# Transposing w for seven heads with VectorE and DMAs in place of TensorE, in a hybrid attention layer

## The chip, the cores and the metric

The kernel runs on one core of one Trainium2 chip. Its time is the device time of one execution in microseconds (us); lower is better. The kernel before takes 351.91 us, the median of three runs (351.11 to 352.12).

## The reference, cut to what matters

A layer over 512 positions with 1024 features, all in f32. The input is normalised and projected; eight heads use stick-breaking attention ("sb") and eight use block attention with slopes ("mb"). With 512 positions and blocks of 256, all past blocks are selected, so an mb head is a causal softmax with a linear position term. Each half of the heads is normalised, gated and projected out, and a gate with a side input closes the layer.

```python
q_sb, k_sb, v_sb, z_sb, q_mb, k_mb, v_mb, z_mb = jnp.split(rmsnorm(x, g_mix) @ w_in, split_at, axis=-1)
# mb head: s = q k^T * scale - slope * (q_pos - k_pos), masked to the past
probs = softmax(s)
out = probs @ v
y_mb = rmsnorm(o_mb, g_out_mb) * silu(z_mb)
x = x + concat([y_sb, y_mb]) @ w_out
x = x + (p @ w_ple) * sigmoid(rmsnorm(x, g_ple) @ w_ple_gate)
return rmsnorm(x, g_final)
```

## The kernel before

Nothing is rounded to fewer bits than needed: each f32 operand of a product is split into a hi part (fp32r, a cast on ScalarE, `part_hi`, L80) and a lo part (VectorE subtracts hi from the source, `part_lo`, L86), and a product is three matmuls, hi hi, hi lo and lo hi (`mul3`, L75). Weights come by DMA into three raw tiles, are split into `wu` tiles (five of them), and the next load is issued when a lo part has freed a raw tile.

TensorE's order is written out by hand. A stream of projection steps (`F`, three matmuls each) runs through the whole attention stage; the work of the heads is put between these steps. A slot belongs to head h (loop at L764): the transposes of head h-1's w, the scores of head h (`scores`, L590, eight matmuls into one three-bank PSUM tile `sc`, which has one buffer), the sums of head h-1 (`sums`, L701), and projection steps between them and after them up to a number `TARGET[h]`. The tail (L816 to L832) does the transposes and sums of head 15 between the last steps.

For an mb head (`front_mb`, L640) VectorE takes the row maxima of scores plus positions (`top`, L648, four operations that read `sc`), ScalarE the exponentials (L656), VectorE the reciprocal of the row sums and four scalings of w by it (`norm`, L664). The positions `rel` are halved per head (L642). w has 1280 columns in 128 partitions: four row blocks, of 512, 384, 128 and 256 columns, the causal part alone. `trans` (L685) transposes ten 128x128 blocks on TensorE into PSUM, in three groups of 4, 4 and 2 blocks, and splits each group into `ph` and `plo`. `sums` multiplies V with both. `turn` (L879) is used in the last stage for x2: VectorE transposes 32x32 blocks within a tile, one DMA writes the tile to DRAM, four DMAs bring it back with the blocks at their transposed places.

The orders of VectorE, ScalarE, GpSimd and SP are not written by hand after the start: a scheduler sets them when the program is built, with its own estimates of when inputs are ready and with priority for some. Each engine runs its row in that order and waits where an input is missing.

Of the kernel before, what the change touches and what calls it, by code (L numbers as in the profile page):

```python
# [20 lines left out]
NH = 8  # L21
# [13 lines left out]
def layer(ctx, tc, x, xT, pT, w_qkz, w_v, gcols, g_final, w_out, w_ple, w_gate, out):  # L35
# [100 lines left out]
    def flush_f():  # L136
        while fq:
            pop_f()
# [221 lines left out]
    def end_v(g, t, ps):  # L360

        ps = ps.rearrange("p (r e d) -> p r e d", r=2, e=2)
        hi = V[g][t][:, :, 0::3, :]
        part_hi(hi, ps, rx["t"][:, t:t + 1])
        for r in range(2):
            part_lo(hi[:, r], V[g][t][:, r, 1:3, :], ps[:, r], rx["t"][:, t:t + 1])
# [273 lines left out]
    def front_mb(h):  # L640
        if h > NH:
            nc.scalar.activation(rel, rel, AF.Copy, scale=0.5)  # L642
# [21 lines left out]
        def norm(i):  # L664
            a, b = rows(i)
            nc.vector.tensor_scalar_mul(w[:, a:b], w[:, a:b], rl[:, i:i + 1])
# [17 lines left out]

    def trans(h, c):  # L685

        w = W[h]
# [76 lines left out]
    for h in range(2 * NH):  # L764
        if h == 0:
            front(0)
        else:
            b = h - 1
            flush_f()
            trans(b, 0)  # L770
            F(1, False)
            front(h)
            F(1, False)
            trans(b, 1)
            F(2, False)
            sums(b, 0)
            trans(b, 2)
            F(2, False)
            sums(b, 1)
            F(2)  # L780
            sums(b, 2)
        F(max(0, TARGET[h] - steps[0]))
        if h == NH + 1:
            row_scale(0)
# [32 lines left out]
    flush_f()  # L817
    trans(b, 0)
    G(2)
    trans(b, 1)  # L820
    G(2)
# [9 lines left out]
    G(21)  # L831
# [47 lines left out]
    def turn(t):  # L879

        y, tt = (raw.tile([P, DM], F32, name=n, tag="raw") for n in ("yb", "xb"))
        yv = y.rearrange("p (b k j) -> p k b j", b=4, j=32)
        for n in range(2):
            nc.vector.transpose(yv[:, 4 * n:4 * n + 4], x2[0][:, t, n * S:(n + 1) * S].rearrange(
                "p (k b j) -> p k b j", b=4, j=32))
        y_d = dram.tile([P, DM], F32, name=f"y_d{t}")
        load(y_d, y)
        src = y_d.rearrange("(a i) (b c) -> b i a c", a=4, b=4)
        for b_ in range(4):
            load(tt[32 * b_:32 * b_ + 32, :].rearrange("i (a c) -> i a c", a=4), src[b_])  # L890
        turned[t] = tt.rearrange("p (a k j) -> p k a j", a=4, j=32)
# [136 lines left out]
```

## Time and profile before

| | |
|---|---|
| median of three runs | 351.91 us |
| profiled execution | 352.3 us |
| its span | 350.5 us |
| TensorE busy | 341.8 us (98%) |
| VectorE busy | 279.6 us (80%) |
| ScalarE busy | 220.6 us (63%) |
| GpSimd busy | 19.6 us (6%) |
| DMA traffic | 43.31 MB, mean 124 GB/s |

PE is TensorE, DVE is VectorE, ACT is ScalarE, POOL is GpSimd. Times in timelines count from the start of the span. Matmul lengths overlap: the price of one is read from start to start. The same holds for VectorE where one operation follows another without a wait. A helper such as `part_lo` records all its operations under one line (L88), so the names of the tiles tell them apart: `wu` is a weight split, `plo` the lo part of a transposed w, `wg` a gate weight split.

### The profile page before, as it was taken

To read this page: it belongs to the slowest core of one execution; us is meant where nothing else is said; L and a number is where in the kernel's file an instruction comes from. 1 tells how busy PE (TensorE), PEld (TensorE's weight loads), DVE (VectorE), ACT (ScalarE), POOL (GpSimd) and SP (SyncE) were. 2 spreads that over 40 slices of the span, in tenths; PEclk is the share of its full clock that TensorE was granted. 3 is DMA by queue.
4 is the path that set the end of the run, shared out by engine and by line. 5 is a ranking of instruction groups with operands and counts; after the bars stand their busy time and mean duration, and the time that the engine had idled before them with its cause. 6 is when DMAs were issued, how large, how long until landed. Compare 5 with 4: busy or idle time off the path is not lost.

```text
span 350.5 us, 4873 instructions
## 1 busy us (share of the span) xinstructions
PE 341.8 (98%) x1688; PEld 285.1 (81%) x1688; DVE 279.6 (80%) x570; ACT 220.6 (63%) x416; POOL 19.6 (6%) x43
## 2 busy tenths in 40 slices
PE   8999999999999999999999999999999999999991
PEld 6788888888888888888888888888888888888891
DVE  3996799878989897989579889989899979274554
ACT  4876767664767364777387689797776753234341
POOL 2013000000000000000000100000000010000111
PEclk9999999999999999999999999999999999999998
DMA  7997815212141114111105301310911680437321
GB/s 201 422 363 236 279 25 216 75 47 66 53 144 38 65 57 152 43 55 63 52 0 180 122 1 60 122 60 4 352 65 59 184 298 29 153 90 239 122 91 60
DMA packets 17624, 43.31 MB, mean 124 GB/s; under 512 B 1856, under 2 KB 3648, under 8 KB 17600
## 3 DMA queue, kind: packets, MB, share of 16 engines
q1 hardware_dynamic: 17456, 42.75, 35.3%
q8 instruction: 13, 0.21, 0.3%
q10 hardware_dynamic: 144, 0.26, 0.2%
q14 instruction: 11, 0.09, 0.1%
HBM read 37.24 MB, written 5.77 MB: 123 GB/s over the span
## 4 chain that ended last, share of the span: by engine, by line
PE 92%; issue 2%; DMA 2%; ACT 1%; DVE 1%; SPq 0%; POOL 0%; POOLq 0%; DVEq 0%; ACTq 0%
PE pj L70 67%; PE sc L70 9%; PE av L70 8%; PE tp L73 6%; PE tp L70 3%; DMA rawh<-in_pT_dram 2%; SPq L158 0%; ACT junk L864 0%; POOL r L99 0%; POOLq L1024 0%; DVE ot L949 0%; ACT ot L991 0%; DVE tmp L914 0%; DVE x L917 0%; DVE pu L88 0%
## 5 line engine op out<-in xcount | busy, mean ns | idle before, releaser
L70 PE MATMUL pj<-hTh,wu 128*128 128x512 f32 x384 | 134.5, 401 | 0.0
L70 PEld LDWEIGHTS pj<-hTh,wu 128*128 128x128 f32 x384 | 72.2, 188 | 13.0
L70 PE MATMUL pj<-hTl,wu 128*128 128x512 f32 x192 | 75.1, 391 | 0.0
L82 ACT CAST wu<-raw 128x512 fp32r<-128x512 f32 x80 | 46.7, 618 | 24.5 <-PE pj L70 21.0
L88 DVE TENSOR_TENSOR wu<-raw,wu 128x512 fp32r<-128x512 f32 x80 | 52.8, 684 | 2.8 <-ACT wu L82 2.6
L70 PE MATMUL pj<-wg,h 128*128 128x512 f32 (+1 forms) x216 | 44.8, 368 | 0.0
L70 PEld LDWEIGHTS pj<-wg,h 128*128 128x128 f32 x216 | 37.4, 188 | 7.4
L70 PEld LDWEIGHTS pj<-hTl,wu 128*128 128x128 f32 x192 | 36.3, 189 | 5.1
L88 DVE TENSOR_TENSOR plo<-tp,ph 128x512 fp32r<-128x512 f32 (+1 forms) x48 | 28.5, 593 | 6.4 <-ACT ph L82 6.1
L82 ACT CAST ph<-tp 128x512 fp32r<-128x512 f32 (+1 forms) x48 | 24.5, 511 | 13.3 <-PE tp L73 13.2
L70 PE MATMUL pj<-wu,yh 128*128 128x512 f32 x96 | 30.9, 403 | 0.0
L70 PE MATMUL pj<-wu,hTh 128*128 128x512 f32 x96 | 30.1, 395 | 0.0
L621 DVE TENSOR_TENSOR_SCAN inc<-A,own 128x512 f32<-128x512 f32 (+3 forms) x32 | 24.7, 809 | 5.4 <-ACT A L616 5.4
L73 PEld LDWEIGHTS tp<-idf,C 128*128 128x128 f32 x160 | 20.4, 140 | 6.1
L73 PE MATMUL tp<-idf,C 128*128 128x128 f32 x160 | 25.2, 272 | 0.0
L70 PE MATMUL sc<-K,QH 128*128 128x512 f32 (+1 forms) x64 | 19.8, 323 | 0.0
L70 PEld LDWEIGHTS pj<-wu,hTh 128*128 128x128 f32 x96 | 17.3, 188 | 3.1
L658 ACT ACTIVATE C<-A,nm 128x512 f32<-128x512 f32 (+3 forms) x32 | 17.8, 558 | 3.2 <-DVE nm L654 3.0
L70 PE MATMUL av<-ph,v 128*128 128x512 f32 (+1 forms) x64 | 19.7, 309 | 0.0
L298 DVE TENSOR_TENSOR ev<-pj,rx 128x512 f32<-128x512 f32 x24 | 16.4, 684 | 3.9 <-PE pj L70 3.8
L70 PE MATMUL av<-plo,v 128*128 128x512 f32 (+1 forms) x64 | 19.1, 324 | 0.0
L70 PE MATMUL sc<-K,QL 128*128 128x512 f32 (+1 forms) x64 | 19.0, 323 | 0.0
(140 smaller groups left out, 554.6 us busy)
## 6 DMA issues: line engine op xcount, KB each, us to landing
raw<-in_w_qkz_dram SPq DMA_DIRECT2D x24, 512.0 KB, 4.0
raw<-in_w_v_dram SPq DMA_DIRECT2D x8, 512.0 KB, 3.4
raw<-in_w_out_dram SPq DMA_DIRECT2D x8, 512.0 KB, 3.7
raw<-in_w_gate_dram SPq DMA_DIRECT2D x8, 512.0 KB, 3.5
xt<-in_xT_dram SPq DMA_DIRECT2D x4, 512.0 KB, 7.5
xs<-in_x_dram SPq DMA_DIRECT2D x4, 512.0 KB, 10.0
pl_d<-pt SPq DMA_DIRECT2D x8, 256.0 KB, 5.5
x<-in_x_dram SPq DMA_DIRECT2D x4, 512.0 KB, 7.1
```

The lines of the kernel that those rows point to most:

```text
L70: nc.tensor.matmul(ps, lhsT=lhsT, rhs=rhs, start=start, stop=stop)
L73: nc.tensor.transpose(ps, src, idf)
L82: nc.scalar.copy(hi, src)
L88: nc.vector.tensor_sub(lo, src, hi.bitcast(F32))
L298: nc.vector.tensor_mul(t, ps, rx["all"])
L621: nc.vector.tensor_tensor_scan(inc[:, c:c + b - a][:, ::-1], keep[:, a:b][:, ::-1], own[:, S - (b - a):][:, ::-1], 0.0, op0=OP.mult, op1=O ...
L658: nc.scalar.activation(w[:, a:b], s[:, a:b], AF.Exp, scale=QKS, bias=nm[:, i:i + 1], accum_out=l[:, i:i + 1])
```

## The change

For heads 8 to 14 (`TURNED`) w is transposed without TensorE. `turn_w` lets VectorE transpose the 32x32 blocks of w into `yw` (four operations of 384, 384, 256 and 256 columns), stores `yw` to DRAM, and loads it in four DMAs into `tw`; `trans` then splits `tw` in SBUF into `ph` and `plo`, blocks 1 and 3 as two operations. The sums of a turned head stand in the slot two after that of its scores, so the slot of head 9 has none and the tail has those of heads 14 and 15. The four scalings of w of a turned head and the halving of `rel` go to GpSimd. V's lo part is taken in one operation for each group in place of two. `turn` uses the same helpers as `turn_w`; what it does is unchanged. `yw` and `tw` share the buffers of the scores' tile and of w (tags A and C).

```diff
--- before.py
+++ after.py
@@ -359,11 +359,9 @@
 
     def end_v(g, t, ps):
 
-        ps = ps.rearrange("p (r e d) -> p r e d", r=2, e=2)
-        hi = V[g][t][:, :, 0::3, :]
-        part_hi(hi, ps, rx["t"][:, t:t + 1])
-        for r in range(2):
-            part_lo(hi[:, r], V[g][t][:, r, 1:3, :], ps[:, r], rx["t"][:, t:t + 1])
+        ps = ps.rearrange("p (h d) -> p h d", d=HD)
+        v = V[g][t].rearrange("p r (e s) d -> p (r e) s d", s=2)
+        split(v[:, :, 0, :], v[:, :, 1, :], ps, rx["t"][:, t:t + 1])
 
     def new_v(g, t):
 
@@ -639,7 +637,7 @@
 
     def front_mb(h):
         if h > NH:
-            nc.scalar.activation(rel, rel, AF.Copy, scale=0.5)
+            nc.gpsimd.tensor_scalar_mul(rel, rel, 0.5)
         sc = scores(h)
         s = at.tile([P, WID], F32, name="A")
         w = W[h] = at.tile([P, WID], F32, name="C")
@@ -663,7 +661,7 @@
 
         def norm(i):
             a, b = rows(i)
-            nc.vector.tensor_scalar_mul(w[:, a:b], w[:, a:b], rl[:, i:i + 1])
+            (nc.gpsimd if h in TURNED else nc.vector).tensor_scalar_mul(w[:, a:b], w[:, a:b], rl[:, i:i + 1])
 
         hi, lo = slice(2, 4), slice(0, 2)
         fq.extend([
@@ -682,8 +680,50 @@
     JS = ((0,), (1, 3), (2,))
     wt = {}
 
+
+    TURNED = range(NH, 2 * NH - 1)
+    NB = {(3, 0): 0, (3, 1): 1, (3, 2): 2, (2, 0): 3, (2, 1): 4, (2, 2): 5, (1, 0): 6, (1, 1): 7, (3, 3): 8, (0, 0): 9}
+    wT = {}
+
+    def turn_blocks(src, dst, pieces):
+
+        dv = dst.rearrange("p (b n j) -> p n b j", b=4, j=32)
+        sv = src.rearrange("p (n b j) -> p n b j", b=4, j=32)
+        for to, of in pieces:
+            nc.vector.transpose(dv[:, to], sv[:, of])
+
+    def turn_move(name, y, tt):
+
+        y_d = dram.tile(list(y.shape), F32, name=name)
+        load(y_d, y)
+        src = y_d.rearrange("(a i) (b c) -> b i a c", a=4, b=4)
+        for b_ in range(4):
+            load(tt[32 * b_:32 * b_ + 32, :].rearrange("i (a c) -> i a c", a=4), src[b_])
+        return tt.rearrange("p (a n j) -> p n a j", a=4, j=32)
+
+    def turn_w(h):
+        y = at.tile([P, WID], F32, name="yw", tag="A")
+        tt = at.tile([P, WID], F32, name="tw", tag="C")
+        turn_blocks(W[h], y, ((slice(0, 3), slice(0, 3)), (slice(3, 6), slice(4, 7)),
+                              (slice(6, 8), slice(8, 10)), (slice(8, 10), slice(3, 8, 4))))
+        wT[h] = turn_move(f"w_d{h}", y, tt)
+
     def trans(h, c):
 
+        if h in TURNED:
+            ph = at.tile([P, S], F32R, name="ph", bufs=2)
+            plo = at.tile([P, S], F32R, name="plo", bufs=2)
+            off, n = {}, 0
+            with tc.high_priority():
+                for j in JS[c]:
+                    first, last, k = NB[j, j], NB[3, j], NT - j
+                    src = wT[h][:, first:last - 1 if last else None:-3] if k > 1 else wT[h][:, first:first + 1]
+                    hi, lo = (x_[:, n:n + k * P].rearrange("p (n a j) -> p n a j", a=4, j=32) for x_ in (ph, plo))
+                    split(hi, lo, src)
+                    off[j] = n
+                    n += k * P
+            wt[c] = ph, plo, off
+            return
         w = W[h]
         tp = pp.tile([P, S], F32, name="tp", bufs=2)
         n, off = 0, {}
@@ -765,20 +805,25 @@
         if h == 0:
             front(0)
         else:
-            b = h - 1
+            b = h - 2 if h - 2 in TURNED else h - 1
             flush_f()
-            trans(b, 0)
-            F(1, False)
-            front(h)
-            F(1, False)
-            trans(b, 1)
-            F(2, False)
-            sums(b, 0)
-            trans(b, 2)
-            F(2, False)
-            sums(b, 1)
-            F(2)
-            sums(b, 2)
+            if h - 1 in TURNED:
+                turn_w(h - 1)
+            if b in TURNED and b == h - 1:
+                front(h)
+            else:
+                trans(b, 0)
+                F(1, False)
+                front(h)
+                F(1, False)
+                trans(b, 1)
+                F(2, False)
+                sums(b, 0)
+                trans(b, 2)
+                F(2, False)
+                sums(b, 1)
+                F(2)
+                sums(b, 2)
         F(max(0, TARGET[h] - steps[0]))
         if h == NH + 1:
             row_scale(0)
@@ -815,10 +860,18 @@
 
     b = 2 * NH - 1
     flush_f()
+    trans(b - 1, 0)
+    trans(b - 1, 1)
+    G(1)
+    sums(b - 1, 0)
+    trans(b - 1, 2)
+    G(1)
+    sums(b - 1, 1)
     trans(b, 0)
+    sums(b - 1, 2)
     G(2)
     trans(b, 1)
-    G(2)
+    G(3)
     sums(b, 0)
     trans(b, 2)
     G(3)
@@ -828,7 +881,7 @@
     flush_f()
     G(8)
     row_scale(1)
-    G(21)
+    G(18)
     flush_late()
 
     gf = at.tile([P, DM], F32, name="gf", tag="B", bufs=1)
@@ -879,16 +932,8 @@
     def turn(t):
 
         y, tt = (raw.tile([P, DM], F32, name=n, tag="raw") for n in ("yb", "xb"))
-        yv = y.rearrange("p (b k j) -> p k b j", b=4, j=32)
-        for n in range(2):
-            nc.vector.transpose(yv[:, 4 * n:4 * n + 4], x2[0][:, t, n * S:(n + 1) * S].rearrange(
-                "p (k b j) -> p k b j", b=4, j=32))
-        y_d = dram.tile([P, DM], F32, name=f"y_d{t}")
-        load(y_d, y)
-        src = y_d.rearrange("(a i) (b c) -> b i a c", a=4, b=4)
-        for b_ in range(4):
-            load(tt[32 * b_:32 * b_ + 32, :].rearrange("i (a c) -> i a c", a=4), src[b_])
-        turned[t] = tt.rearrange("p (a k j) -> p k a j", a=4, j=32)
+        turn_blocks(x2[0][:, t, :], y, [(slice(4 * n, 4 * n + 4),) * 2 for n in range(2)])
+        turned[t] = turn_move(f"y_d{t}", y, tt)
 
     turned = {}
```

The order of instructions at two places follows, with the names as the program builds them; the numbers behind a name are buffer numbers, and line numbers of the changed program are its own. First place: the slot of head 12, VectorE before. `plo_2316` is the first lo part of head 11, `sc_2323` the scores of head 12, L650 takes maxima, `ev` is the scaled copy of a projection.

```order
L88 TENSOR_TENSOR plo_2316<-tp_2310,ph_2315 128x512
L650 ISA A_2332,m_2334<-sc_2323,rel_439 128x512
L650 ISA m_2334 128x1
L650 ISA A_2332,m_2334<-sc_2323,rel_439 128x384
L650 ISA m_2334 128x1
L298 TENSOR_TENSOR ev_2341<-pj_2268,rx_360 128x512
L654 TENSOR_SCALAR nm_2335<-m_2334 128x2
L88 TENSOR_TENSOR plo_2363<-tp_2357,ph_2362 128x512
```

VectorE in the changed program, same slot: ahead of the maxima (L648) of head 12, and the first of them.

```order
L660 RECIPROCAL rl_2175<-l_2174 128x2
L298 TENSOR_TENSOR ev_2308<-pj_2222,rx_360 128x512
L660 RECIPROCAL rl_2175<-l_2174 128x2
L693 STREAM_TRANSPOSE yw_2270<-C_2171 128x3x4x32
L648 ISA A_2299,m_2301<-sc_2290,rel_439 128x512
```

And from the last maximum (`sc_2290` are the scores of head 12) to the parts of head 10: `tw_2142` is w^T of head 10, `yw_2270` the turned blocks of head 11.

```order
L648 ISA A_2299,m_2301<-sc_2290,rel_439 128x256
L648 ISA m_2301 128x1
L315 TENSOR_TENSOR QL0_2312<-ev_2308,QH0_2310 64x512
L652 TENSOR_SCALAR nm_2302<-m_2301 128x2
L315 TENSOR_TENSOR QL1_2313<-ev_2308,QH1_2311 64x512
L693 STREAM_TRANSPOSE yw_2270<-C_2171 128x3x4x32
L693 STREAM_TRANSPOSE yw_2270<-C_2171 128x2x4x32 x2
L88 TENSOR_TENSOR wu_2368<-raw_2107,wu_2368 128x512 x2
L88 TENSOR_TENSOR plo_2283<-tw_2142,ph_2282 128x512
L88 TENSOR_TENSOR plo_2325<-tw_2142,ph_2324 128x384
L88 TENSOR_TENSOR plo_2325<-tw_2142,ph_2324 128x128
L88 TENSOR_TENSOR plo_2347<-tw_2142,ph_2346 128x256
```

The first lo part stood ahead of the maxima and belonged to the head before; now head 10's stands behind the maxima, two QL, three rows of transposes and two weight splits, and a scaled copy of a projection (`pj_2222`) stands ahead of the maxima.

TensorE before, same slot: from the last score matmul to the sums of head 11 with `ph_2315` and `plo_2316`.

```order
L70 MATMUL sc_2323<-K0_2262,QL0_2160 128x256
L70 MATMUL pj_2268<-hTh_138,wu_1894 128x512
L70 MATMUL pj_2268<-hTl_139,wu_1894 128x512
L70 MATMUL pj_2268<-hTh_138,wu_1894 128x512
L73 MATMUL tp_2357<-idf_126,C_2211 128x128 x4
L70 MATMUL pj_2355<-hTh_138,wu_1995 128x512
L70 MATMUL pj_2355<-hTl_139,wu_1995 128x512
L70 MATMUL pj_2355<-hTh_138,wu_1995 128x512 x2
L70 MATMUL pj_2355<-hTl_139,wu_1995 128x512
L70 MATMUL pj_2355<-hTh_138,wu_1995 128x512
L70 MATMUL av_2379<-ph_2315,v_1694 128x512
L70 MATMUL av_2379<-plo_2316,v_1694 128x512
```

TensorE in the changed program: from the last score matmul to the sums of head 10 with `ph_2282` and `plo_2283`.

```order
L70 MATMUL sc_2290<-K0_2216,QL0_2117 128x256
L70 MATMUL pj_2222<-hTh_138,wu_1878 128x512
L70 MATMUL pj_2222<-hTl_139,wu_1878 128x512
L70 MATMUL pj_2222<-hTh_138,wu_1878 128x512
L70 MATMUL pj_2322<-hTh_138,wu_1962 128x512
L70 MATMUL pj_2322<-hTl_139,wu_1962 128x512
L70 MATMUL pj_2322<-hTh_138,wu_1962 128x512 x2
L70 MATMUL pj_2322<-hTl_139,wu_1962 128x512
L70 MATMUL pj_2322<-hTh_138,wu_1962 128x512
L70 MATMUL av_2343<-ph_2282,v_1686 128x512
L70 MATMUL av_2343<-plo_2283,v_1686 128x512
```

The four transposes (`tp`) are gone; the three steps between scores and sums are the same, and the first of them holds the last matmuls of `pj_2222`.

Second place: the tail, VectorE before, up to the first lo part of head 15 (`plo_2832`).

```order
L666 TENSOR_SCALAR C_2739<-C_2739,rl_2743 128x256
L422 SCALAR_TENSOR_TENSOR x2_2542<-pj_2747,r0_2035,x2_2542 128x512
L88 TENSOR_TENSOR wu_2711<-raw_2548,wu_2711 128x512
L90 SCALAR_TENSOR_TENSOR wg01_2879<-raw_2714,gc_102,wg01_2879 128x512
L724 TENSOR_TENSOR o_2815<-av_2772,tmp_2816 64x512
L422 SCALAR_TENSOR_TENSOR x2_2542<-pj_2790,r0_2035,x2_2542 128x512
L90 SCALAR_TENSOR_TENSOR wg01_2879<-raw_2714,gc_102,wg01_2879 128x512
L88 TENSOR_TENSOR plo_2832<-tp_2826,ph_2831 128x512
```

VectorE in the changed program, up to the first lo part of head 14 (`plo_2791`), which the first sums of the tail read.

```order
L420 SCALAR_TENSOR_TENSOR x2_2497<-pj_2747,r0_1993,x2_2497 128x512
L660 RECIPROCAL rl_2706<-l_2705 128x2 x2
L664 TENSOR_SCALAR C_2702<-C_2702,rl_2706 128x128
L664 TENSOR_SCALAR C_2702<-C_2702,rl_2706 128x512
L664 TENSOR_SCALAR C_2702<-C_2702,rl_2706 128x256
L664 TENSOR_SCALAR C_2702<-C_2702,rl_2706 128x384
L764 TENSOR_TENSOR o_2645<-av_2732,tmp_2772 64x512
L90 SCALAR_TENSOR_TENSOR wg01_2860<-raw_2768,gc_102,wg01_2860 128x512 x2
L782 TENSOR_TENSOR acc_2254<-acc_2254,tmp_2778 128x512
L783 TENSOR_TENSOR o_2645<-o_2645,szg6_2040 128x512
L88 TENSOR_TENSOR yl6_2780<-o_2645,yh_2779 128x512
L88 TENSOR_TENSOR plo_2791<-tw_2673,ph_2790 128x512
```

The scalings of head 15 (L664), a sum of o (L764), the gate splits and three operations on o (L782, L783, L88) now stand ahead of the lo part that the tail's first sums read; before, the tail's first sums are head 15's.

## Rows read from the trace of the kernel before

**Rows 1.** The page: TensorE's busy time, and the chain by engine.
```profile
PE 341.8 (98%) x1688; PEld 285.1 (81%) x1688; DVE 279.6 (80%) x570; ACT 220.6 (63%) x416; POOL 19.6 (6%) x43
...
PE 92%; issue 2%; DMA 2%; ACT 1%; DVE 1%; SPq 0%; POOL 0%; POOLq 0%; DVEq 0%; ACTq 0%
```

**Rows 2.** Busy time by stretch: length, PE, PEld, DVE, ACT, POOL; then clock, DMA share.
```profile
189.34:272.24 82.90, 82.90 (x434) 69.87 (x432) 75.95 (x199) 63.27 (x138) 2.24 (x4) 1.00 0.28 99
```

**Rows 3.** Timeline of TensorE: start, length, operation; four transposes among matmuls.
```profile
202.25 0.39 PE L70 MATMUL pj<-hTh,wu 128*128 128x512 f32 x1
202.48 0.60 PE L73 MATMUL tp<-idf,C 128*128 128x128 f32 x4
202.83 0.48 PE L70 MATMUL pj<-hTh,wu 128*128 128x512 f32 x1
203.15 0.39 PE L70 MATMUL pj<-hTl,wu 128*128 128x512 f32 x1
```

**Rows 4.** Timeline of TensorE: one projection step, and later the scores of head 12.
```profile
222.36 0.62 PE L70 MATMUL pj<-hTh,wu 128*128 128x512 f32 x2
222.82 0.39 PE L70 MATMUL pj<-hTl,wu 128*128 128x512 f32 x1
223.04 0.39 PE L70 MATMUL pj<-hTh,wu 128*128 128x512 f32 x1
...
224.41 0.40 PE L70 MATMUL sc<-K,QH 128*128 128x512 f32 x1
...
225.69 0.40 PE L70 MATMUL pj<-hTh,wu 128*128 128x512 f32 x1
```

**Rows 5.** Timeline of VectorE: single operations, two lines between dots where spacing is read.
```profile
202.60 0.55 DVE L650 CUSTOM_DVE_ANT_0 A<-sc,rel 128x384 f32<-128x384 f32 x1
...
203.08 0.29 DVE L650 CUSTOM_DVE_ANT_0 A<-sc,rel 128x128 f32<-128x128 f32 x1
...
203.29 0.17 DVE L654 TENSOR_SCALAR nm<-m 128x2 f32<-128x2 f32 x1
203.36 0.42 DVE L650 CUSTOM_DVE_ANT_0 A<-sc,rel 128x256 f32<-128x256 f32 x1
203.70 0.08 DVE L650 DVE_READ_ACCUMULATOR2_ANT m<- 128x1 f32 x1
...
211.20 0.68 DVE L88 TENSOR_TENSOR wu<-raw,wu 128x512 fp32r<-128x512 f32 x1
211.79 0.68 DVE L743 TENSOR_TENSOR o<-o,szg 128x512 f32<-128x512 f32 x1
...
230.94 1.42 DVE L315 TENSOR_TENSOR QL<-ev,QH 64x512 fp32r<-64x512 f32 x2
...
255.74 1.28 DVE L666 TENSOR_SCALAR C<-C,rl 128x512 f32<-128x512 f32 x4
...
295.21 1.29 DVE L884 STREAM_TRANSPOSE yb<-x 128x512 f32<-128x512 f32 x2
```

**Rows 6.** Groups by line and shape: ScalarE's copies of Q.
```profile
L313 ACT CAST QH<-ev 64x512 fp32r<-64x512 f32 x16 | 9.9, 620 | 2.3 <-DVE ev L298 2.2
```

**Rows 7.** Groups by line and shape: GpSimd's select over 512 columns.
```profile
L585 POOL TENSOR_SCALAR_AFFINE_SELECT rel<-rel 128x512 f32<-128x512 f32 x1 | 0.6, 613 | 0.1
```

**Rows 8.** DMA issues with size and time to landing: a turned tile out, and back.
```profile
y_d<-yb SPq DMA_DIRECT2D x3, 512.0 KB, 3.6
xb<-y_d SPq DMA_DIRECT2D x12, 128.0 KB, 2.8
```

**Rows 9.** Timelines of GpSimd and VectorE: a power alone, and one beside gate splits.
```profile
200.62 1.02 POOL L99 TENSOR_TENSOR r<-rs_t,mhalf 128x4 f32<-128x4 f32 x1 [11.10 <-DVE rs_t L98]
...
287.26 1.37 POOL L99 TENSOR_TENSOR r<-rs_t,mhalf 128x4 f32<-128x4 f32 x1 [72.77 <-DVE rs_t L98]
...
287.02 1.41 DVE L90 SCALAR_TENSOR_TENSOR wg<-raw,gc,wg 128x512 fp32r<-128x512 f32 x2
288.67 1.41 DVE L422 SCALAR_TENSOR_TENSOR x<-pj,r,x 128x512 f32<-128x512 f32 x2 [0.24 <-POOL r L99]
```


## Prediction

> **What bounds the kernel now.** I read the busy times and the chain of the page first: TensorE is busy 98% of the span and holds 92% of the chain that ended last [rows 1]. The table by stretches comes next. From the maxima of head 9 to the first lo part of head 15 (189.3 to 272.2 us) TensorE has no idle time, VectorE is busy 75.95 of 82.90 us (92%), ScalarE 76%, GpSimd 3% [rows 2]. So what leaves TensorE there is gained, as long as VectorE, which has 8% to spare, hands over in time. The timelines of the engines give the price of one instruction, and the order of the changed program tells what stands ahead of what.
>
> **What TensorE loses.** Four transposes take 0.35 us from start to start, and the matmul behind them 0.32 in place of 0.23, so 0.44 us [rows 3]; a head has two such groups and one of two blocks (taken as half): 1.10 us. Seven heads make 7.7 us. The sums of heads 8 to 14 move one slot later: the slot with the scores of head 9 has none, the tail has two, which costs TensorE nothing by itself. If nobody waits, 352.3 us of the profiled execution become 344.6.
>
> **What VectorE gets.** Two neighbouring 512-column operations start 0.60 us apart (0.59 in the row), 384 columns take 0.48, 256 take 0.34, 128 take 0.21, an operation on 64 partitions 0.71 (two of them 1.42) [rows 5], and one with a scalar beside two tiles 0.66 behind its like (two gate lo parts 1.41 with the last one's end) [rows 9]. The two 512-column block transposes took 1.29 us together, so they cost what other operations of their width do [rows 5]. A turned head adds transposes of 384, 384, 256 and 256 columns, 1.64 us, and loses the four scalings, 1.28 us [rows 5]. The lo part of blocks 1 and 3 is cut in two (384 and 128 columns), +0.09. So +0.45 us a head, six heads in the stretch: 2.7 us, of 6.95 that were idle. V's single lo pass takes off some 0.2 us for each of 16 calls, where TensorE waited for nobody: I count 0, and at most 1 us of gain if the queue starts head 9 earlier. Halving rel off ScalarE frees 0.62 us a head there: 0, since ScalarE has a quarter to spare [rows 2]. By totals VectorE would just keep up. The loss is in the order.
>
> **Where TensorE has to stand.** After the scores of head h TensorE runs three projection steps of 0.68 us (three matmuls, 222.36 to 223.04) and then wants the hi and lo part of head h-2: 2.04 us after the end of the scores [rows 4]. The four maxima read the scores, so VectorE cannot begin them earlier; they and one small operation between them take 0.61 + 0.48 + 0.21 + 0.07 + 0.34 = 1.71 us [rows 5]. Whatever else stands between the scores and that lo part in VectorE's fixed row delays TensorE, however fast VectorE was before. I take 0.1 us for a hand-over between engines, an estimate, as the rows do not give one alone. Four places count:
> - Scores of head 11. The second QL stands ahead of the maxima. It needs the projection that ended 1.6 us before the scores (seven matmuls), its scaled copy (0.60), three copies on ScalarE (1.9, each 0.62 and a gap) [rows 6] and itself (0.71), 3.4 us with hand-overs, against 1.6 + 1.28 for the scores (224.41 to 225.69 in [rows 4]): maxima 0.5 late. Then maxima 1.71, one o sum 0.71, one weight lo 0.60, a small one 0.07, the lo part 0.60: 4.2. Less 2.04: 2.1 us.
> - Scores of head 12, first place shown with the change. Ahead of the maxima stands a scaled copy of a projection whose last step TensorE runs after the scores (0.68 + 0.1 + 0.60), a reciprocal 0.1 and a transpose 0.48. Then maxima 1.71, two QL 1.42, transposes 0.48 and 0.68, two weight lo 1.20, the lo part 0.60. Together 8.05; less 2.04: 6.0 us. Before, that lo part stands ahead of the maxima.
> - Scores of head 15. The maxima come 0.4 late behind an x2 sum (0.66), an o sum, two weight lo and two transposes; after them two transposes 0.75 with the small one, an x2 sum 0.66, the lo part 0.60: 4.1. Less 2.04: 2.1 us.
> - Tail, second place shown. From the scores of head 15 to the first lo part of head 14 VectorE has 0.4 + 14.5 us to do: maxima 1.71, transposes 0.75, four lo parts 1.63, three x2 sums 1.98, two weight lo 1.20, four gate lo 2.66, two reciprocals 0.2, the four scalings of head 15 1.28, o sum 0.71, three operations on o 1.80, the lo part 0.60. TensorE arrives after ten steps and the sums of head 13, 6.8 + 1.3, plus the 2.1 above: 10.2. Stand: 4.7 us.
> In the slots of heads 10, 13 and 14 the lo part stands ahead of the maxima or close behind: under 1 us each, left to the range.
> Sum: 352.3 - 7.7 + 2.1 + 6.0 + 2.1 + 4.7 = 359.5 us. The profiled execution lies 0.4 above the median of the runs (351.91), so 359.1.
>
> **Costs that the trace does not show.** GpSimd's scaling: nothing like it runs before. From below 0.61 us for 512 columns, the affine select [rows 7]; from above twice that. A transpose that stands right behind its reciprocal waits for it, 0.7 us, at some six places: 0 to 5 us. I take 0, because most lie ahead of scores that are late anyway, and keep 5 for the range. The way of w^T: 512 KB out took 3.6 us to land, 128 KB back 2.8 [rows 8]; 640 KB, and four loads behind each other at 0.4 us, make some 9 us (estimate). In the tail 12 us of VectorE's row lie between the last transpose of head 14 and its lo part, of which hi needs 0.6: hidden, by 2 us. But SP issues the four loads behind a gate load, and that waits for a weight lo that stands 4 us behind the transposes. Without that cover: up to 3 us. Loads of weights that now stand behind w's store in SP's queue: VectorE's row splits them a slot or more ahead of use, 0, up to 2 if not.
>
> **A rule that speaks against it.** A GpSimd power of 4 columns took 1.02 us alone and 1.37 us while VectorE made a gate lo part from two SBUF operands, and VectorE then waited 0.24 us for it [rows 9]. The Trainium skill, page "SBUF — State Buffer", section "Who interferes with whom", says that a GpSimd instruction that reads SBUF and a VectorE one with two SBUF inputs share a port which the first to start holds for its whole length. The rows agree for GpSimd as the loser; none shows VectorE losing. The changed kernel puts 35 GpSimd instructions that read SBUF beside VectorE, whose lo parts of w now read two SBUF tiles in place of PSUM. As a mechanism: 28 scalings and 7 halvings are some 7 x 2.1 = 15 us of GpSimd at 1.2 ns a column; if VectorE loses half, and half of that falls between scores and sums, it is 4 us more: 363. It is a rival with its own chance.
>
> **Rivals.** (1) Faster, 344.6 to 350.8: the stands sum to under 6.5 us. For that VectorE's 22.5 us of rows in the two large places must run in two thirds of the time, or TensorE must meet fewer of them; for it speaks that the totals nearly fit (2.7 us more against 6.95 idle), that V's pass and GpSimd take work off, and that a maximum may start when its own two score matmuls are through, up to 0.8 us earlier at each place. Against it, the row is fixed and I used back-to-back spacings. Middle 348. (2) No change: stands equal to 7.7 us, the head 12 place alone and little more: 352. (3) The port: 363. (4) w^T late in the tail or the waits for GpSimd: 3 to 5 us more, 362 to 364.
>
> **How the numbers follow.** Forecast (354 to 362): 0.57. Rival 1: 0.17. Rival 2: 0.06. Rival 3: 0.10. Rival 4: 0.10. Slower than by 0.3%, which is about what a measurement of this kernel can tell from none: 0.77; faster by more 0.17; within 0.06. The range 349 to 366 leaves out most of rival 1 and the far end of 3 and 4; the forecast's own is 354 to 362.
>
> **What would show it.** TensorE idle in front of the sums of head 10 for about 6 us, put down to VectorE's lo part, and in front of those of head 14 for about 5; smaller ones at heads 9 and 13. VectorE busy above 90% with the transposes at 0.5 to 0.7 us. No wait of the sums for a DMA. The gaps of the transposes gone, 1.1 us a slot. Wrong, if TensorE shows no idle there, or if VectorE's time ahead of those lo parts is spent waiting for GpSimd or a DMA.

## The result, and the profile after

The changed kernel takes 393.83 us (391.48 to 395.85) against 351.56 for the kernel before: ratio 1.1199, interval 1.1133 to 1.1266. It is 42 us slower where 7 were forecast, and above the range of 349 to 366. The profiled execution took 391.48 us with a span of 389.4.

The page of the changed kernel: busy times, TensorE's busy tenths and granted clock in 40 slices, and the chain by engine, against [rows 1].

```profile
PE 347.5 (89%) x1618; PEld 286.7 (74%) x1618; DVE 284.8 (73%) x561; ACT 218.2 (56%) x416; POOL 64.9 (17%) x78
...
PE   8999999999999999999799592974877599999992
...
PEclk9999999999999999999699897998698699999997
...
PE 73%; DVE 13%; POOL 6%; issue 4%; ACT 4%; POOLq 0%; DVEq 0%; ACTq 0%
```

TensorE fell from 98% to 89% of the span; its busy time is 5.7 us longer although 70 transposes are gone; the chain now holds VectorE 13%, GpSimd 6%, ScalarE 4%. The loss lies in slices 20 to 32, and in seven of the same slices the granted clock is below full.

A stand is time in which TensorE has to wait. Timeline of TensorE in the changed kernel, the ten instructions behind a stand of more than 0.3 us (in brackets the idle time and its releaser); before, the heads' stretch has none [rows 2].

```profile
187.82 0.77 PE L70 MATMUL pj<-hTh,wu 128*128 128x512 f32 x1 [2.83 <-DVE v L90]
...
220.47 0.47 PE L70 MATMUL av<-ph,v 128*128 128x512 f32 x1 [3.43 <-DVE nm L652]
...
221.65 0.80 PE L70 MATMUL av<-plo,v 128*128 128x512 f32 x1 [0.71 <-DVE plo L88]
...
237.71 0.49 PE L70 MATMUL av<-ph,v 128*128 128x512 f32 x1 [3.83 <-ACT ph L82]
...
241.40 0.80 PE L70 MATMUL av<-plo,v 128*128 128x512 f32 x1 [3.20 <-DVE plo L88]
...
253.77 0.50 PE L70 MATMUL av<-ph,v 128*128 128x512 f32 x1 [0.49 <-ACT ph L82]
...
256.57 0.50 PE L70 MATMUL av<-plo,v 128*128 128x512 f32 x1 [2.30 <-DVE plo L88]
...
274.08 1.22 PE L70 MATMUL pj<-wu,yh 128*128 128x512 f32 x2 [7.34 <-DVE x L420]
...
292.56 0.50 PE L70 MATMUL av<-plo,v 128*128 128x512 f32 x1 [3.38 <-DVE plo L88]
...
306.35 0.79 PE L70 MATMUL av<-ph,v 128*128 128x512 f32 x1 [6.09 <-ACT ph L82]
```

They sum to 33.6 us. Six of them stand at the prediction's four places (sums of head 9: 220 and 222; 10: 238 and 241; 13: 293; 14: 306), 4.1, 7.0, 3.4 and 6.1 us. Four do not: ahead of the scores of head 9 (188), at the sums of head 11 (254 and 257), and at the projection out (274).

TensorE's clock around the first stand, by stretches (length, busy time of each engine, then the granted clock).

```profile
core 0: us, PE busy (x) PEld busy (x) DVE busy (x) ACT busy (x) POOL busy (x), PEclk, DMA share, GB/s
181.20:184.60 3.40, 3.40 (x16) 2.82 (x15) 2.65 (x5) 1.59 (x4) 0.43 (x1) 1.00 0.11 45
187.82:193.72 5.90, 5.89 (x16) 4.94 (x17) 4.98 (x16) 2.44 (x6) 0.52 (x1) 0.50 0.84 282
194.30:200.00 5.70, 5.70 (x26) 4.69 (x25) 3.33 (x8) 3.02 (x9) 5.54 (x5) 1.00 0.61 150
```

Behind 2.83 us without work TensorE ran 5.9 us at a granted clock of 0.50, the lower of its two levels (1.2 and 2.4 GHz): 16 matmuls in 5.9 us, and then 26 in 5.7 us. So a stand costs more than its length. The sum is: 350.5 - 7.7 (transposes) + 33.6 (stands) + 13.4 (busy time of 347.5 less 341.8 - 7.7, the matmuls at the lower clock) = 389.8, against a span of 389.4. The 13.4 is what is left over, but the trace bears it out: behind these stands TensorE works some 25 us at a granted clock of 0.50, and half of that is 12.6.

Where the first stand comes from. GpSimd and then VectorE in the changed kernel, head 8's scalings (L664) and transposes (L693).

```profile
176.71 1.51 POOL L664 TENSOR_SCALAR C<-C,rl 128x128 f32<-128x128 f32 x2 [1.86 <-DVE rl L660]
178.84 2.79 POOL L664 TENSOR_SCALAR C<-C,rl 128x512 f32<-128x512 f32 x2 [0.62 <-DVE rl L660]
```

```profile
176.45 0.17 DVE L660 RECIPROCAL rl<-l 128x2 f32<-128x2 f32 x1
178.25 0.45 DVE L693 STREAM_TRANSPOSE yw<-C 128x256 f32<-128x256 f32 x1 [1.64 <-POOL C L664]
...
180.44 0.58 DVE L693 STREAM_TRANSPOSE yw<-C 128x384 f32<-128x384 f32 x1 [1.31 <-POOL C L664]
181.66 0.58 DVE L693 STREAM_TRANSPOSE yw<-C 128x384 f32<-128x384 f32 x1 [0.65 <-POOL C L664]
182.27 0.70 DVE L764 TENSOR_TENSOR o<-av,tmp 64x512 f32<-64x512 f32 x1
```

The first reciprocal starts at 176.45; GpSimd scales from 176.7 to 181.6; VectorE's row has the transposes close behind the reciprocals, so it waits 1.64, 1.31 and 0.65 us, and the sum of o, V's lo part and the weight splits behind them come late. The group of GpSimd's 512-column scaling, and the whole of this wait:

```profile
L664 POOL TENSOR_SCALAR C<-C,rl 128x512 f32<-128x512 f32 x7 | 12.2, 1746 | 14.4 <-DVE rl L660 14.4
```

```profile
DVE yw L693 <- POOL C L664: 16.8, 16, 1.8
```

512 columns took 1.75 us, not the 0.61 of the select [rows 7] nor twice that; VectorE, which scaled all four blocks in 1.28 us [rows 5] and seven heads in 9.0, now waits 16.8 us at 16 places.

### The profile page after: what moved, and what is told of

Read it like the earlier page. It is cut to its first block, busy times and chain, and to the rows that moved or that the text cites. A ratio compares the mean times of both kernels' runs of the same rounds, so it can differ in the third digit from the quotient of the medians.

```text
span 389.4 us, 4838 instructions
## 1 busy us (share of the span) xinstructions
PE 347.5 (89%) x1618; PEld 286.7 (74%) x1618; DVE 284.8 (73%) x561; ACT 218.2 (56%) x416; POOL 64.9 (17%) x78
## 4 chain that ended last, share of the span: by engine, by line
PE 73%; DVE 13%; POOL 6%; issue 4%; ACT 4%; POOLq 0%; DVEq 0%; ACTq 0%
PE pj L70 53%; PE sc L70 7%; PE av L70 7%; POOL C L664 6%; PE tp L73 3%; PE tp L70 3%; DVE A L648 2%; DVE yw L693 2%; DVE wu L88 1%; DVE plo L88 1%; ACT C L656 1%; DVE o L764 1%; DVE K L323 1%; DVE x L420 1%; DVE o L783 1%
## 5 line engine op out<-in xcount | busy, mean ns | idle before, releaser
L88 DVE TENSOR_TENSOR wu<-raw,wu 128x512 fp32r<-128x512 f32 x80 | 52.9, 689 | 1.8 <-ACT wu L82 1.6
L70 PE MATMUL pj<-wu,yh 128*128 128x512 f32 x96 | 33.1, 428 | 7.3 <-DVE x L420 7.3
L664 POOL TENSOR_SCALAR C<-C,rl 128x128 f32<-128x128 f32 (+3 forms) x28 | 31.3, 1131 | 33.1 <-DVE rl L660 33.1
L70 PE MATMUL av<-ph,v 128*128 128x512 f32 (+1 forms) x64 | 21.5, 336 | 13.8 <-ACT ph L82 10.4
L312 POOL MEMSET QL<- 64x512 f32 x16 | 8.2, 522 | 147.5 <-PE sc L70 130.8
L70 PE MATMUL av<-plo,v 128*128 128x512 f32 (+1 forms) x64 | 21.5, 361 | 9.6 <-DVE plo L88 9.6
L70 PEld LDWEIGHTS pj<-wu,yh 128*128 128x128 f32 x96 | 19.0, 207 | 11.2 <-DVE x L420 7.8
L99 POOL TENSOR_TENSOR r<-rs_t,mhalf 128x1 f32<-128x1 f32 (+1 forms) x10 | 8.2, 823 | 110.1 <-DVE rs_t L98 110.1
L70 PEld LDWEIGHTS av<-ph,v 128*128 128x128 f32 x64 | 13.3, 207 | 17.4 <-ACT ph L82 11.7
L693 DVE STREAM_TRANSPOSE yw<-C 128x256 f32<-128x256 f32 (+1 forms) x28 | 13.7, 503 | 16.9 <-POOL C L664 16.8
L82 ACT CAST ph<-tw 128x512 fp32r<-128x512 f32 (+3 forms) x28 | 11.5, 456 | 24.1 <-DVE plo L88 15.6
L70 PEld LDWEIGHTS av<-plo,v 128*128 128x128 f32 x64 | 13.3, 207 | 13.8 <-DVE plo L88 11.8
```

What stands on the lines that cost most here:

```text
L70: nc.tensor.matmul(ps, lhsT=lhsT, rhs=rhs, start=start, stop=stop)
L82: nc.scalar.copy(hi, src)
L88: nc.vector.tensor_sub(lo, src, hi.bitcast(F32))
L99: nc.gpsimd.tensor_tensor(dst, t[:, :width], mhalf[:, :width], op=OP.pow)
L312: nc.gpsimd.memset(Ql[e][other].bitcast(F32), 0.0)
L664: (nc.gpsimd if h in TURNED else nc.vector).tensor_scalar_mul(w[:, a:b], w[:, a:b], rl[:, i:i + 1])
```

## Experiments

Theory S: GpSimd's scalings make VectorE wait in its fixed row. Theory O: what the prediction said, lo parts behind the maxima make the stands, whoever scales. Each time is a median of its own runs; the kernel before, run beside them, took 351.1 to 351.4.

**V's lo part alone.** The kernel before with the change's `end_v`.

```diff
-            part_lo(hi[:, r], V[g][t][:, r, 1:3, :], ps[:, r], rx["t"][:, t:t + 1])
+        split(v[:, :, 0, :], v[:, :, 1, :], ps, rx["t"][:, t:t + 1])
```

> The kernel before with one part of the change alone: V's lo part in one operation of 256 columns in place of two of 128. Theory S (scalings on GpSimd make VectorE wait in its fixed row): nothing waits for V's lo here, 351.6 within 1 us, TensorE without idle time ahead of the scores of head 9. Rival V (the one longer operation frees its bank later and makes TensorE stand 2.83 us ahead of the scores of head 9): that stand shows here too, with some us of half clock behind it, 356 to 358.

Measured 351.26, ratio 1.0003 (0.9993 to 1.0012), no stand. This part costs nothing; the 2.83 us are not V's.

**Scalings on GpSimd alone**, TensorE still transposes.

```diff
-            nc.vector.tensor_scalar_mul(w[:, a:b], w[:, a:b], rl[:, i:i + 1])
+            (nc.gpsimd if h < 2 * NH - 1 else nc.vector).tensor_scalar_mul(...)
```

> The kernel before with the four scalings of w of heads 8 to 14 on GpSimd, TensorE still transposing. Theory S: four scalings take 4.3 us in place of 1.28, but VectorE has nothing in its row that waits for them; TensorE's transposes do. They stood 0.5 to 2 us behind the last scaling, so up to 3 us of stand in some slots: 353 to 360. Theory O (the order of VectorE's row, the lo part behind the maxima, makes the stands, whoever scales): the row is the one of before, 350.5 to 352.5. Theory P (GpSimd and VectorE lose by running side by side): VectorE's own operations get longer in the heads' stretch, mean of the 512-column lo part over 0.72 us.

Measured 359.55, ratio 1.0237 (1.0221 to 1.0252). Here it is not VectorE but TensorE's transposes that stand for GpSimd, 5.7 us in all. The move of the scalings loses by itself, as S says.

**Scalings taken back from GpSimd**, the rest of the change kept: on VectorE (e3), on ScalarE (e4).

```diff
-            (nc.gpsimd if h in TURNED else nc.vector).tensor_scalar_mul(w[:, a:b], ...)
+            nc.vector.tensor_scalar_mul(w[:, a:b], ...)                            # e3
+            nc.scalar.activation(w[:, a:b], w[:, a:b], AF.Copy, scale=rl[:, i:i + 1])  # e4
```

> The changed kernel with the four scalings back on VectorE; its row stays nearly the same otherwise, the lo parts still behind the maxima. Theory S: VectorE's 16.8 us of waiting for GpSimd go, 9 us of scalings come: the stand ahead of the scores of head 9 (2.83) and the one ahead of the projection out (7.34) vanish, and most of the half clock behind them, 358 to 368. Theory O: the stands at heads 9, 10, 13 and 14 stay as they are and the others come from the same order, 383 or more.

> The changed kernel with the four scalings of the turned heads on ScalarE, which was busy 76% of this stretch before. Theory S: no wait of VectorE for GpSimd and no scalings in its row, some 1.8 us a head more on ScalarE: 352 to 362. Theory O: 383 or more, the stands at heads 9, 10, 13 and 14 as large as in the changed kernel. Theory A (any engine that scales outside VectorE makes VectorE wait by the hand-over, since the transposes stand right behind the reciprocal): VectorE waits 8 us or more for ScalarE's scalings, 365 to 380.

Measured 376.10 (1.0714; 1.0691 to 1.0736) and 372.55 (1.0625; 1.0578 to 1.0673). Both lie between theories S and O: 18 to 21 of the 42 us go with GpSimd's scalings, the rest does not. The second time lies in the range of theory A, but VectorE waited only 2.4 us for ScalarE's scalings, so the hand-over alone is not it. The halving of rel stays on GpSimd in both; what it costs was not tested apart. Timeline of TensorE with the scalings on VectorE, the stands at the prediction's four places:

```profile
212.46 0.47 PE L70 MATMUL av<-ph,v 128*128 128x512 f32 x1 [1.50 <-DVE nm L652]
...
213.64 0.78 PE L70 MATMUL av<-plo,v 128*128 128x512 f32 x1 [0.71 <-DVE plo L88]
...
229.13 0.50 PE L70 MATMUL av<-ph,v 128*128 128x512 f32 x1 [3.06 <-ACT ph L82]
...
233.67 0.79 PE L70 MATMUL av<-plo,v 128*128 128x512 f32 x1 [4.04 <-DVE plo L88]
...
280.58 0.50 PE L70 MATMUL av<-plo,v 128*128 128x512 f32 x1 [2.23 <-DVE plo L88]
...
290.89 0.50 PE L70 MATMUL av<-ph,v 128*128 128x512 f32 x1 [2.62 <-ACT ph L82]
```

Heads 9 (2.2), 10 (7.1), 13 (2.2) and 14 (2.6, and 0.3 behind it): 14.5 us, where the prediction has 14.9 and the changed kernel 20.6. With the scalings on ScalarE the same places have 2.1, 6.1, 1.7 and 3.9, 13.8 us. The stand at 188 is gone; at head 11 1.8 of 2.8 us are left and at the projection out 4.0 of 7.3, so these two are only in part GpSimd's. So O holds for the four places that the prediction named, though not for the time, and S for 13.3 us of stands and 2 of half clock on top.

**What GpSimd costs VectorE.** The same 28 scalings, added to the kernel before, of a tile that is no longer read.

```diff
+            if h < 2 * NH - 1:
+                nc.gpsimd.tensor_scalar_mul(own[:, :b - a], own[:, :b - a], rl[:, i:i + 1])
```

> The kernel before, with the same 28 scalings on GpSimd added, but of a tile that nobody reads any more; VectorE scales w as before and no engine waits for the added work. It tells GpSimd's own price and what VectorE loses beside it. Theory S: GpSimd takes 1.5 to 1.8 us for 512 columns, and the time stays 351.2 within 1 us. Theory P (the two engines hinder each other in SBUF): VectorE's busy time from head 9 to head 15 rises from 76 us by 3 or more, TensorE stands, 354 to 362.

Measured 352.14, ratio 1.0015 (1.0000 to 1.0031). GpSimd's group, and the stretch of heads 9 to 15 (columns as above) in this kernel and in the kernel before:

```profile
L668 POOL TENSOR_SCALAR own<-own,rl 128x512 f32<-128x512 f32 x7 | 12.6, 1793 | 37.3 <-DVE rl L662 37.3
```

```profile
189.00:272.00 83.00, 82.89 (x432) 69.57 (x431) 79.34 (x198) 63.45 (x138) 33.16 (x27) 1.00 0.27 98
```

```profile
189.00:272.00 83.00, 83.00 (x433) 69.92 (x432) 76.07 (x199) 63.37 (x139) 2.58 (x4) 1.00 0.28 100
```

1.79 us again, with nobody waiting for it: the price comes with the operation and not with the order of the changed kernel. VectorE's busy time rose from 76.1 to 79.3 us (4%), and TensorE did not stand for it. This is the kernel before, whose lo parts of w read PSUM. In the changed kernel, where they read two SBUF tiles, VectorE's busy time is 284.8 us with the scalings on GpSimd and 283.7 with them on ScalarE, for the same 561 instructions: 1.1 us. So VectorE lost little by the shared port. GpSimd can have lost by it: single scalings of 512 columns took up to 2.47 us in the changed kernel, where the mean is 1.75.

**Two stands made on purpose.**

```diff
+    N3, N6 = 11, 18
...
+            for _ in range({3: N3, 6: N6}.get(h, 0)):
+                nc.gpsimd.tensor_scalar_mul(idf, idf, 1.0)
```

> The kernel before with two artificial stands of TensorE: between two groups of transposes in the slots of heads 3 and 6 GpSimd multiplies the identity by one, 11 and 18 times, and the second group waits for it. If one takes 0.3 to 0.6 us, the stands are 0.6 to 4 and 2.7 to 8 us. Theory C (a stand costs more than its length, since TensorE comes back at the lower clock): behind each stand over 2 us the matmuls start 0.43 us apart in place of 0.23 for some microseconds, and the time is 351.2 plus the stands plus 2 to 4 us for each. Theory L (only the length counts, the rest of the loss in the changed kernel lies elsewhere): 351.2 plus the stands, within 1 us.

Measured 373.51, ratio 1.0623 (1.0587 to 1.0659). TensorE at the stands, and by stretches behind them:

```profile
94.61 0.69 PE L73 MATMUL tp<-idf,C 128*128 128x128 f32 x2 [5.93 <-POOL idf L774]
...
157.72 0.69 PE L73 MATMUL tp<-idf,C 128*128 128x128 f32 x2 [11.41 <-POOL idf L774]
```

```profile
94.61:97.50 2.89, 2.88 (x9) 2.50 (x10) 1.11 (x2) 1.73 (x3) 0.41 (x1) 0.50 0.00 0
157.72:161.00 3.28, 3.28 (x10) 2.80 (x11) 1.23 (x3) 0.59 (x1) 0.00 (x0) 0.50 0.00 0
```

The stands are 17.3 us, longer than foreseen, and the clock was 0.50 for 2.9 us behind the first and some 4.6 behind the second, of which the row shows 3.3. The span grew by 19.8, so half clock cost 2.5. Theory C is right in kind, since length alone (theory L) gives 17.3, but its price was too high: by the span 1.2 us for a stand, not 2 to 4. (The medians differ by 22.1 us: the profiled execution lies 1.4 below the median here, and 0.9 above that of the runs beside it in the kernel before.) The price behind a stand is less than in the changed kernel, where some stretches at 0.50 were longer.

**Early transposes, early sum of o, x by its own queue**, one on top of the other, scalings on ScalarE.

```diff
-                turn_w(h - 1)
+                with tc.high_priority():                         # e5
+                    turn_w(h - 1)
-                nc.vector.tensor_add(o[a], av[a], t[a])
+                with tc.high_priority():                         # e9
+                    nc.vector.tensor_add(o[a], av[a], t[a])
-                load(x2[0][:, t, :], x[t * P:(t + 1) * P, :])
+                nc.gpsimd.dma_start(x2[0][:, t, :], ...)         # e12
```

> As the version with the scalings on ScalarE (372.6 us), but the 32x32 transposes have priority in VectorE's row: w^T comes back earlier, and the lo part of head 10 stands two operations behind the first maximum of head 12, in place of behind all four, two QL, the transposes and two weight splits. Theory O (the place of the lo part behind the maxima makes the stands that are left): the stand at the sums of head 10 (6.1 us) falls to under 2, all stands together from 20 to 5 to 10, and the half clock with them: 355 to 364. Theory T (VectorE's total is the bound: it has more work than TensorE in these slots, whatever the order): the stands move to other places, sum 15 to 20, 366 to 374.

Measured 371.53 (1.0563; 1.0533 to 1.0593), in T's range. Head 10's lo part was in time, and TensorE stood as long for something else, the sum of o that frees the one bank of the sums:

```profile
229.79 0.76 PE L70 MATMUL av<-ph,v 128*128 128x512 f32 x1 [5.93 <-DVE o L767]
```

> As the version with scalings on ScalarE and early transposes (371.5 us), and the sum of o, which frees the one PSUM bank of the sums, has priority too: TensorE stood 5.93 us for it at the sums of head 10. Theory W (a few late operations in VectorE's row make the stands, each can be moved away): that stand falls below 2 and nothing takes its place, 360 to 366. Theory T (VectorE has more work than TensorE in these slots, 78.8 us against 76.4 by the rows of before): other operations come late in its place, sum of stands 14 to 20 again, 367 to 374.

Measured 366.09 (1.0429; 1.0384 to 1.0475), between the two ranges; all stands together are 16.1 us, as T has it. This stand fell to two of 1.9 together (1.16 and 0.70), and the one at the projection out is the largest. The sum of x in VectorE's row, and TensorE, which waits for it:

```profile
255.26 0.75 DVE L420 SCALAR_TENSOR_TENSOR x<-pj,r,x 128x512 f32<-128x512 f32 x1 [0.30 <-DMA x<-in_x_dram]
...
256.07 0.80 PE L70 MATMUL pj<-wu,yh 128*128 128x512 f32 x1 [7.64 <-DVE x L420]
```

SP's DMA queue in this kernel, and in the kernel before, where x comes back:

```profile
245.53 0.34 SPq L158 DMA_DIRECT2D w_d<-yw  x1
245.92 4.76 SPq L158 DMA_DIRECT2D tw<-w_d  x5
250.77 2.13 SPq L158 DMA_DIRECT2D x<-in_x_dram  x4
```

```profile
244.39 2.08 SPq L158 DMA_DIRECT2D x<-in_x_dram  x4
```

TensorE's last matmul on the tile that x overwrites began at 241.0 here and 242.6 before; the loads were issued 9.7 and 1.8 us later, since here the store of w, which waits for VectorE, and five loads of w^T stand ahead of them. But VectorE's row, which has this sum behind maxima and lo parts, reached it only 0.30 us before x landed.

> As the version before it for heads 8 to 14 (366.1 us: scalings on ScalarE, early transposes and sum of o), but x comes back for the projection out through GpSimd's DMA queue in place of SP's. There the four loads stood behind the store of one head's w and the loads of w^T, and were issued at 250.8 us, 9.4 us after the last matmul that reads the tile they overwrite (241.4); before it was 1.9 us. Theory Q (SP's queue makes the stand of 7.64 us at the projection out): the stand falls below 2 and most of the half clock behind it goes, 355 to 360. Theory T (VectorE's total): x is there, but its sum comes late in VectorE's row all the same, or others do: 362 to 367. Below 351 by no theory: VectorE's work is 2.4 us over TensorE's, and the tail's stand of 3.3 us stays.

Measured 367.32 (1.0434; 1.0372 to 1.0496). The stand at the projection out is gone, as theory Q has it, and the time is not lower. Q alone is not shown by this: in this version the first sum of x also stands ahead of the maxima in VectorE's row (248.27), so queue and row changed together. VectorE's sum, what the chain of waits now holds in the stand's place, and SP's queue:

```profile
248.27 0.75 DVE L420 SCALAR_TENSOR_TENSOR x<-pj,r,x 128x512 f32<-128x512 f32 x1 [2.29 <-PE sc L70]
```

```profile
246.40 8.62 DMA tw<-w_d
```

```profile
237.53 1.28 SPq L158 DMA_DIRECT2D tw<-w_d  x3
246.01 0.34 SPq L158 DMA_DIRECT2D w_d<-yw  x1
246.40 9.84 SPq L158 DMA_DIRECT2D tw<-w_d  x5
```

TensorE stands 5.04 us for w^T. Three of its quarters were issued from 237.5 us on; the last stands in SP's queue behind the next head's store, which waits for VectorE's transposes, and was issued at 246.40. It then took 8.62 us to land, with x's 2 MB in flight, where a quarter takes 4.4 in the median of the changed kernel. ScalarE, held by a late product of o, was free 0.16 us before it landed, so VectorE's row would have allowed little more. All stands together are 13.1 us, 3.0 less than in the version before it, but TensorE is busy 342.3 us in place of 338.3. T's time (362 to 367) is all but met, and not for T's reason alone: the wait that ends last here is that for w^T, in SP's queue and on its way.

**Other heads.** Heads 1, 3, 5 (e8, e10), 1 to 6 (e11), 1 to 5 (e13) are turned in place of 8 to 14; these need no scaling and have no maxima. rel stays on ScalarE, V's lo part is one operation, transposes have priority, and the tail is that of the kernel before; from e10 on the sum of o has priority too.

```diff
-    TURNED = range(NH, 2 * NH - 1)
+    TURNED = (1, 3, 5)
+            due = [h - 2] * (h - 2 in TURNED) + [h - 1] * (h - 1 not in TURNED)
+            for k_, b in enumerate(due):
...
+                else:
+                    F(4, False)                                  # e10, e11, e13
-                F(2)
+                F(2 - k_)                                        # e8, e10, e11
+                F(3 - 2 * k_)                                    # e13
                 sums(b, 2)
```

> Another choice of heads: w^T of heads 1, 3 and 5 by VectorE and DMAs, two slots behind, the transposes with priority; no scaling is needed there, rel stays on ScalarE, V's lo part in one operation. VectorE was busy 80 to 90% of 16.8 us in these slots and no maxima stand between scores and lo parts. If the loss comes from order and waits (theories S and O), three heads save 3 x 1.10 us: 347.5 to 349.5. If turning loses wherever it stands (VectorE gets 1.73 us for 1.10 us of TensorE): 351 to 358.

Measured 359.53 (1.0230; 1.0210 to 1.0249), outside both ranges. Three stands, 3.75, 2.61 and 1.73 us, all for the bank of the sums in slots that hold two heads; the first:

```profile
97.96 0.47 PE L70 MATMUL av<-ph,v 128*128 128x512 f32 x1 [3.75 <-DVE o L764]
```

> Heads 1, 3 and 5 turned as before (359.5 us), but where one slot holds the sums of two heads four more projection steps stand between them and the sum of o has priority: TensorE stood there 3.75, 2.61 and 1.73 us, each time for the sum of o that frees the bank of the sums. Theory W: the stands go, 3 x 1.10 us and nothing else is left: 347.5 to 349.5. Theory T (turning loses through VectorE's total): VectorE is busy 14 of 17 us here, so it should not bind; if it does, 351 to 356.

Measured 349.53, ratio 0.9939 (0.9916 to 0.9963); stands left 0.5 us.

> Heads 1 to 6 turned, spaced and with priority likewise: each slot from the third to the seventh holds one head's sums, so the bank is free in time; VectorE gets 1.73 us in every slot (14.2 + 1.7 = 15.9) and TensorE loses 1.10 (16.7 - 1.1 = 15.6). Theory W: 6 x 1.10 us, 344.5 to 346.5. Theory T: VectorE is just over TensorE's time, some 0.3 us a slot and stands with half clock: 347 to 356.

Measured 349.34, ratio 0.9943 (0.9923 to 0.9962): twice the heads, no more gain; five stands of 0.71 to 1.24 us, three of them for the third lo part.

> Heads 1 to 5 turned, with one more projection step ahead of the last group's sums, where heads 1 to 6 left stands of 0.78, 0.77 and 1.09 us for the third lo part. Five heads save 5.5 us. If these stands are a matter of place (theory W): 346 to 348. If VectorE's total makes them (15.9 us of work in a slot of 15.6): they come back elsewhere, 348.5 to 350.5.

Measured 348.20, ratio 0.9904 (0.9870 to 0.9939), between the two ranges: it beats the kernel before by 3 us, the best found. Its page, and one slot (columns as above):

```profile
PE 336.7 (97%) x1638; PEld 280.6 (81%) x1638; DVE 285.1 (82%) x579; ACT 220.9 (64%) x421; POOL 20.5 (6%) x43
```

```profile
118.00:135.00 17.00, 17.00 (x81) 14.27 (x80) 16.93 (x32) 10.59 (x21) 0.52 (x1) 1.00 0.65 214
```

TensorE's busy time is 5.1 us less than in the profile of the kernel before and 3.7 less than in that of e1, whose TensorE does the same work (340.4); 5 x 1.10 is 5.5. Two stands of 0.7 and 0.4 us are left. VectorE is busy 96.4 of 102 us (94%) in the six slots from 50 to 152 us, and 16.9 of 17 in the one shown. So turning a head can pay where VectorE is nearly full, if its lo part is early. These heads differ from 8 to 14 in more than their place (no scaling, no maxima), and the runs do not take these differences apart.

## Why the prediction was wrong

The profiled execution took 391.5 us, 32.0 more than the 359.5 of the sum. Of this, 18.7 us are stands over the 14.9 that the sum has, and 13.4 are matmuls at the lower clock.

- **Transposes, 7.7 us less: right in kind.** Five heads took 3.7 to 5.1 off TensorE's busy time, where the sum has 5.5 (e13); seven were not measured by themselves.
- **The four places of the order, 14.9 us: right in the main.** In the changed kernel they are 20.6. With the scalings on VectorE they are 2.2, 7.1, 2.2 and 2.9, with the scalings on ScalarE 2.1, 6.1, 1.7 and 3.9, against 2.1, 6.0, 2.1 and 4.7 in the sum. That the sum with VectorE (14.5) comes so near is in part luck, since VectorE has seven heads' scalings there that the forecast did not count. And at head 14 the wait that ends last is not for the lo part, as forecast, but for the hi part: in the changed kernel ScalarE makes it behind a product of o, and waits 2.0 us for VectorE to make that o.
- **GpSimd's scaling: the step that failed first.** It was bounded by 0.61 us for 512 columns and twice that, from a select that reads no scalar per partition and was the nearest row; the waits behind it were taken as 0, at most 5 us. The scaling took 1.75, VectorE waited 16.8 us, and with the scalings elsewhere 18 to 21 us of the loss were gone (e3, e4). The Trainium skill, page "GPSIMD Engine Reference", section "3.1 Elementwise — side-by-side cycle accounting", has GpSimd at about half VectorE's speed for an f32 addition of two tiles. Here the measurement, four scalings in 4.28 us against 1.28, is worse. The upper bound should have been three times the select. With it the waits become a chain: the transposes stand close behind the reciprocal in a row that cannot be overtaken, so every late scaling delays what is behind, V's lo part and x2 sums included. That made the stand at 188 and lengthened those at 254 to 257 (by 1.0 us) and 274 (by 3.3); the prediction left head 11 "to the range" and had neither of the other two. The sign that it gave for being wrong, VectorE waiting for GpSimd, is what the trace shows.
- **The lower clock had no term.** 13.4 us of the loss, and still some 11 with the scalings on VectorE. Before, the granted clock of this stretch is 1.00 [rows 2], so nothing there prices it; still, a forecast of 15 us of stands in four places needed a line for what TensorE does behind them.
- **"By totals VectorE would just keep up": too kind.** The 6.95 us of idle time were counted in the stretch of before, but the change shortens it by 6.6: VectorE's 76.1 + 2.7 = 78.8 us meet 76.4. That this lack of slack made the stands is argued and not shown. A removed stand came back elsewhere in e5 and e12, but e9 gained 5.4 us, e13 gained with VectorE at 94%, and in e9 VectorE is busy 76.65 us of the 91 from 189 to 280 (columns as above) and waits in its row for the rest:

```profile
189.00:280.00 91.00, 75.83 (x348) 61.57 (x346) 76.65 (x198) 70.36 (x160) 14.55 (x9) 0.96 0.58 176
```

- **Rivals.** The port: VectorE lost 3.3 us of busy time in the kernel before and TensorE none (e6), and 1.1 us in the changed one. w^T late: in the changed kernel ScalarE waited 0.7 us for it, since VectorE was later still; with VectorE's waits for GpSimd gone, loads that stand behind the store of w in SP's queue came late (e9: x; e12: a quarter of w^T, for which TensorE stood 5.04 us), more than the 2 to 3 us given. The range ended at 366: it had a few us for each of these costs and none for the lower clock.

What stays open: whether heads 8 to 14 can be turned without loss at all, and whether VectorE's total or the order of its row binds there. The best of them took 366 us with 16.1 us of stands and 4.2 of half clock, and no experiment turned fewer of them.

## What to carry to other kernels

Work that is moved from the bounding engine to one that is 92% busy is no sure gain: check the shortened stretch against that engine's new total, and read its fixed row, and the DMA queue's, for what stands behind each new wait. Where an engine has not run an operation, let its price range to three times the nearest row, and price a stand of TensorE with the matmuls at half clock behind it. Choose the places: the same trade on five other heads, 1 to 5, gained 3 us.

## What the runs showed of the hardware

GpSimd's halving of 512 columns took 1.49 us beside two VectorE operations that read PSUM, and 3.06 beside weight and w lo parts that read two SBUF tiles (changed kernel, GpSimd):

```profile
219.89 3.06 POOL L640 TENSOR_SCALAR rel<-rel 128x512 f32<-128x512 f32 x1 [1.60 <-DVE m L648]
...
273.53 1.49 POOL L640 TENSOR_SCALAR rel<-rel 128x512 f32<-128x512 f32 x1 [8.63 <-DVE m L648]
```

VectorE's negation of two columns took 0.16 us, and 0.57 while GpSimd halved (1.79 us from 193.79 on):

```profile
193.13 0.16 DVE L652 TENSOR_SCALAR nm<-m 128x2 f32<-128x2 f32 x1
194.15 0.57 DVE L652 TENSOR_SCALAR nm<-m 128x2 f32<-128x2 f32 x1
```

The Trainium skill, page "SBUF — State Buffer", section "Who interferes with whom", has the two share a port that one holds at a time. These rows agree. The loser is mostly GpSimd: VectorE's first lo parts of a turned w took 685 ns with GpSimd scaling and 682 with ScalarE scaling.
